# Zero products ahead of x, fewer transfers for S5's matrices, and half of the turn tables on GpSimd, in a two-layer encoder on one core

## The chip, the cores and the metric

The kernel runs on one core of a Trainium2 chip. The metric is the device time of one execution in microseconds (us); lower is better. Three runs of the kernel before took 1330.01 to 1330.89 us, median 1330.19. A profiled execution of its own is read for everything else.

## The reference

The input x has 256 tokens of 1024 channels, in float32. Two layers follow each other, and a last RMSNorm. Each layer is

```
x += 0.5 * swiglu(rms_norm(x), ffn1)                 # width 2816
h  = rms_norm(x);  split h @ w_in into S5, GLA and GQA columns
y  = [S5(u), gated linear attention, grouped-query attention]
x += (sum_b sigmoid(h @ w_merge_gate + b)_b * (y_b @ w_branch_b)) @ w_out
x += 0.5 * swiglu(rms_norm(x), ffn2)
```

The S5 branch is a linear recurrence in both directions, with 32 groups of 16 channels and 64 complex states a group: lam_bar = exp(lam dt), b_bar = (lam_bar - 1) / lam * b, state <- lam_bar * state + b_bar u, y = Re(c state). The sizes of the projections, not this recurrence, make most of the arithmetic.

## The kernel before, in words

**Products.** TensorE multiplies in a form that takes operands split into two parts. Each weight chunk (128 partitions x 2 x 512, a tile `raw`, five buffers) is loaded by SyncE's queue (L220), cast by ScalarE into `hi` (L224), and VectorE subtracts to give `lo` (L225). Three products follow for each 128x512 block: act_hi x hi (L234), act_hi x lo (L235), act_lo x hi (L236). Activations reach TensorE as hTh and hTl, made from transposes of x (class Norm, `half`). Ffn blocks are 512 columns wide, and their evacuation runs through ScalarE (L300, L306) and VectorE (L301, L307).

**Order.** Each engine executes its own list in order, and so does each DMA queue. A scheduler with a timing model lays these lists out at build time, from the order of the program, dependencies and priorities. `weave` interleaves the work that prepares S5's tables (`s5_tables`) with feed-forward layers: layer 0's with ffn1 of layer 0, layer 1's with ffn2 of layer 0 and ffn1 of layer 1.

**Start.** Under high priority the constructor issues loads of x, of the first norm's gain (`vec`) and again of x, on ScalarE's queue but for one. ScalarE also loads an activation table and runs one activation named `warm`. TensorE transposes the gain (`pv`, L189) and x (`pt`, L1169), and then the first weights products come.

**S5 tables.** `s5_params` computes powers of lam_bar, and 16 GpSimd copies (L490, L491) place one set of them as `lpb`. `s5_tables` loads the matrices B (`bn`) and C (into tiles `U`, L542), transposes C on TensorE (`cT`, L548) and copies it on ScalarE to `cq` (real, imaginary, minus imaginary). Then four quarters of 8 groups follow, in the order 1, 2, 3, 0. For each, VectorE makes `bb` (input matrices), `cc` (output matrices) and `e` (turn factors exp(i theta n), outer products of the two tables `ef` and `eg`) by complex products: four multiplications into temporaries (`T` or `U`), a subtraction and an addition, each 128x512 (`cmul_steps`, L350 to L359). GpSimd writes the decay part of `e` (L605) and four copies `kx` (L615). Quarters 1, 2 and 3 are stored in DRAM (`scr`, L612, L618) by SyncE's queue. The pool that holds `bb`, `cc` and `e` has one buffer of `e`, so the next quarter's first write to `e` waits until the store of the last has landed.

Of the kernel before, what the change touches and what calls it, by code (L numbers as in the profile page):

```python
# [9 lines left out]
F32 = mybir.dt.float32  # L10
F32R = mybir.dt.float32r
AF = mybir.ActivationFunctionType
ALU = mybir.AluOpType
AX = mybir.AxisListType

P = 128
# [12 lines left out]
NQ = 4  # L29
# [96 lines left out]
class Enc:  # L126
    def __init__(self, tc, ctx, ins, out):
        self.tc, self.nc, self.ctx, self.ins, self.out = tc, tc.nc, ctx, ins, out
        nc = self.nc
        pool = lambda name, bufs, **kw: ctx.enter_context(tc.tile_pool(name=name, bufs=bufs, **kw))  # L130
        self.const = pool("const", 1)
        self.wraw = pool("wraw", WBUFS[0])
        self.whl = pool("whl", WBUFS[1])
        self.hp = pool("hp", 1)
        self.st = pool("st", 2)
        self.pmm = pool("pmm", 3, space=bass.MemoryType.PSUM)
        self.psm = pool("psm", 3, space=bass.MemoryType.PSUM)
        self.ptr = pool("ptr", 2, space=bass.MemoryType.PSUM)
        self.n = self.ahead_by = 0
        c = self.const  # L140
        self.ident = c.tile([P, P], F32, name="ident")
        make_identity(nc, self.ident)
        self.x = c.tile([P, NT, D], F32, name="x")
        self.cst = c.tile([P, C_MIX], F32, name="cst")
        self.row = {}
        self.mhalf = c.tile([P, 32], F32, name="mhalf")
        nc.gpsimd.memset(self.mhalf, -0.5)

        nc.scalar.activation(c.tile([P, 1], F32, name="warm"), self.mhalf[:, :1], AF.Silu)
        with tc.high_priority():  # L150
            xd = lambda eng, t, h: eng.dma_start(self.x[:, t, h * 512:(h + 1) * 512],
                                                 ins["x"][0, t * P:(t + 1) * P, h * 512:(h + 1) * 512])
            xd(nc.scalar, 0, 0)
            xd(nc.sync, 1, 0)
            self.vectors("ffn1_norm", eng=nc.scalar)
            for t in range(NT):
                xd(nc.scalar, t, 1)
        self.ld = pool("s5ld", 1)
        self.ahead, self.small = {}, {}
        self.scr = {(l, q): tc.dram_tile([P, SCR], F32, name=f"scr{l}_{q}") for l in range(DEPTH) for q in range(NQ)}  # L160
# [4 lines left out]

    def t2(self, shape, dt=F32, ring="ra"):
        return self.phase.tile(shape, dt, name=self.nm("t"), tag=ring, bufs=self.rings[ring])

    def vectors(self, *names, eng=None):

# [113 lines left out]
    def ffn(self, l, which, nm, nxt):  # L284

        nc, ins = self.nc, self.ins
        wg, wu, wd = (ins[f"{which}_w_{s}"][l] for s in ("gate", "up", "down"))
        with self.tc.tile_pool(name=f"ffn{which}{l}", bufs=1) as fp:
            self.phase, self.rings = fp, {"ra": 4}
            if nm.at == 0:  # L290
                nm.half(0)
            act, rstd = nm.act, nm.rstd
            sh = fp.tile([P, KF, SEQ], F32R, name=f"sTh{which}{l}")
            sl = fp.tile([P, KF, SEQ], F32R, name=f"sTl{which}{l}")

            def evac(b):
                def f(t, ps):
                    self.n += 1
                    sg, s = self.t2([P, 256]), self.t2([P, 256])
                    nc.scalar.activation(sg, ps[:, :256], AF.Silu, scale=rstd[:, t:t + 1])  # L300
                    nc.vector.scalar_tensor_tensor(s, ps[:, 256:], rstd[:, t:t + 1], sg, op0=ALU.mult, op1=ALU.mult)  # L301
                    pt = self.ptr.tile([P, 2, P], F32, name=f"st{self.n}", tag="tr")
                    for j in range(2):
                        nc.tensor.transpose(pt[:, j], s[:, j * P:(j + 1) * P], self.ident)  # L304
                    h = sh[:, 2 * b:2 * b + 2, t * P:(t + 1) * P]
                    nc.scalar.copy(h, pt)  # L306
                    nc.vector.tensor_tensor(sl[:, 2 * b:2 * b + 2, t * P:(t + 1) * P], pt, h.bitcast(F32),  # L307
                                            op=ALU.subtract)
                return f

            blocks = []
            for b in range(KF // 2):
                cs = slice(b * 256, (b + 1) * 256)
                blocks.append((cols((wg, cs), (wu, cs)), 512, evac(b)))
            yield from self.stream(act, KD, blocks, lead=2, hooks={0: nm.finish}, fine=(l, which) == (0, "ffn1"))
            nm2 = self.nxt = nxt()
            last = isinstance(nm2, Final)

            def down(c):
                def f(t, ps):  # L320
                    xs = self.x[:, t, c * 512:(c + 1) * 512]
                    nc.vector.scalar_tensor_tensor(xs, ps, 0.5, xs, op0=ALU.mult, op1=ALU.add)
                    if last:
                        nm2.half(c, t)
                return f

            sact = lambda k, t: (sh[:, k, t * P:(t + 1) * P], sl[:, k, t * P:(t + 1) * P])
            yield from self.stream(sact, KF, [(cols((wd, slice(c * 512, (c + 1) * 512))), 512, down(c))
                                              for c in range(2)],
                                   hooks=() if last else {-(-KF // WCH) + 1: lambda: nm2.half(0)},  # L330
                                   tail=3 * WCH if last else None)
# [80 lines left out]
    def s5_params(self, l, c):  # L412
        nc, ins = self.nc, self.ins
# [14 lines left out]
        ps = self.psm.tile([P, 3, w], F32, name="lmT", tag="sm")  # L428
# [9 lines left out]
        dt, r1, cs, sn, a = (pp.tile([P, w], F32, name=f"pq{i}") for i in range(5))  # L438
# [15 lines left out]
        for i, (x, y) in {2: (1, 1), 3: (2, 1), 4: (2, 2)}.items():  # L454
            self.cmul(pw[:, 0, i], pw[:, 1, i], pw[:, 0, x], pw[:, 1, x], pw[:, 0, y], pw[:, 1, y], T)
        qo = lambda a: a.rearrange("p (q e a) -> p q e a", q=NQ, e=2)
        po = lambda a: a.rearrange("p (q a e) -> p q e a", q=NQ, e=2)
# [25 lines left out]
        pb = pp.tile([P, 2, 4, w], F32, name="pb")  # L483
# [1 line left out]
        back = [x.unsqueeze(1).to_broadcast((P, 4, w)) for x in (cs, a)]  # L485
        self.cmul(pb[:, 0], pb[:, 1], pw[:, 0, :4], pw[:, 1, :4], back[0], back[1],
                  [x.rearrange("p w f -> p (w f)").rearrange("p (f w) -> p f w", f=4) for x in T8])
        for i in range(2):
            for t in range(4):
                nc.gpsimd.tensor_copy(po(self.lpb[:64, i, t]), qo(pb[:64, i, 3 - t]))  # L490
                nc.gpsimd.tensor_copy(po(self.lpb[64:, i, t]), qo(pb[64:, i, t]))  # L491
        v.tensor_scalar(sn, sn, self.tab(C_SGN, 1), None, op0=ALU.mult)
        yield

# [20 lines left out]
    def s5_tables(self, l, pp):  # L515
        nc, ins = self.nc, self.ins
# [13 lines left out]
        cn = [T2[i].rearrange("p g c -> p (g c)").rearrange("p (t r) -> p t r", t=4) for i in range(2)]  # L530
        cq = pp.tile([P, 3, NQ, P], F32, name="cq")
        for i, s in enumerate(("re", "im")):
            bn = pp.tile([P, G, 16], F32, name=self.nm("bn"))
            b.append(bn)
            for d in range(2):
                nc.sync.dma_start(bn[d * 64:(d + 1) * 64], ins[f"s5_b_{s}"][l, d].rearrange("g p f -> p g f"))
            for d in range(2):
                for e in range(2):
                    for h in range(2):
                        for ii in range(2):  # L540
                            r = e * 64 + h * 32 + ii * 16
                            nc.sync.dma_start(  # L542
                                cn[i][r:r + 16, :, d * 64:(d + 1) * 64],
                                ins[f"s5_c_{s}"][l, d].rearrange("(h q i e) f p -> e h i f q p", q=NQ, e=2, h=2)[e, h, ii])
        for i in range(2):
            ps = self.psm.tile([P, 4, P], F32, name=self.nm("cT"), tag="sm")
            for t in range(4):
                nc.tensor.transpose(ps[:, t], cn[i][:, t], self.ident)  # L548
            nc.scalar.copy(cq[:, i], ps)
            if i == 1:  # L550
                nc.scalar.activation(cq[:, 2], ps, AF.Copy, scale=-1.0)
        yield
        T = [pp.tile([P, GQ, 4, 16], F32, name=f"T{i}") for i in range(4)]
        for q in (1, 2, 3, 0):
# [14 lines left out]
            for i in range(2):  # L569
                ps = self.psm.tile([P, 4, P], F32, name=self.nm("bT"), tag="sm")  # L570
# [15 lines left out]
            for i in range(2):  # L586
                for a in range(4):
                    for d in range(2):
                        rows = slice(d * 64, (d + 1) * 64)
                        lt = bb[rows, i, 2 * a:2 * a + 2].rearrange("p e f -> p (e f)")  # L590
                        nc.tensor.matmul(kp[d][a * 32:(a + 1) * 32, :, 1 - d:4 - d], lt, c5[rows, i, :, a, d:d + 3],
                                         start=i == 0, stop=i == 1)
# [8 lines left out]
            g8 = [self.eg[:, i, gs].unsqueeze(3).to_broadcast((P, GQ, 8, 8)) for i in range(2)]  # L601
            e8 = [E[:, i].rearrange("p g (a b) -> p g a b", a=8) for i in range(2)]
            tt = [T2[i].rearrange("p g (a b) -> p g a b", a=8) for i in range(4)]
            yield from self.cmul_steps(e8[0], e8[1], f8[0], f8[1], g8[0], g8[1], tt)
            nc.gpsimd.tensor_tensor(ld["e"][:, SCR_R - SCR_E:].rearrange("p (g c) -> p g c", g=GQ),  # L605
                                    self.r4[:, gs].unsqueeze(2).to_broadcast((P, GQ, 64)),
                                    self.tab(C_RM, 64).unsqueeze(1).to_broadcast((P, GQ, 64)), op=ALU.mult)
# [666 lines left out]
```

## Time and profile before

| | |
|---|---|
| median of three runs | 1330.19 us (1330.01 to 1330.89) |
| the profiled execution | 1329.67 us, its span 1327.9 |
| TensorE products (PE) | 1295.5 us busy, 98% |
| VectorE (DVE) | 1000.0 us, 75% |
| ScalarE (ACT) | 699.2 us, 53% |
| GpSimd (POOL) | 86.7 us, 7% |
| DMA | 249.87 MB, mean 188 GB/s |

The span runs from the first to the last recorded instruction; the execution's own time has 1.8 us more. "Busy" is the union of an engine's instructions. PEld is TensorE's weight load, which lies beside products. Products overlap in the pipeline, so their start times, not their durations, show the rate. In the timeline an arrow reads "output <- inputs", "x8" counts instructions that one row joins, and the bracket at a row's end is the time that the engine stood idle before it and what it waited for. SPq and ACTq are the issue of transfers on SyncE's and ScalarE's queue.

### The profile page before, as it was taken

To read this page: it belongs to the slowest core of one execution; us is meant where nothing else is said; L and a number is where in the kernel's file an instruction comes from. 1 tells how busy PE (TensorE), PEld (TensorE's weight loads), DVE (VectorE), ACT (ScalarE), POOL (GpSimd) and SP (SyncE) were. 2 spreads that over 40 slices of the span, in tenths; PEclk is the share of its full clock that TensorE was granted. 3 is DMA by queue.
4 is the path that set the end of the run, shared out by engine and by line. 5 is a ranking of instruction groups with operands and counts; after the bars stand their busy time and mean duration, and the time that the engine had idled before them with its cause. 6 is when DMAs were issued, how large, how long until landed. Compare 5 with 4: busy or idle time off the path is not lost.

```text
span 1327.9 us, 19275 instructions
## 1 busy us (share of the span) xinstructions
PE 1295.5 (98%) x6792; PEld 1049.2 (79%) x6792; DVE 1000.0 (75%) x1798; ACT 699.2 (53%) x1132; POOL 86.7 (7%) x109
## 2 busy tenths in 40 slices
PE   8999999999999999999999999999999999999997
PEld 6788778878787788788888778887787868888886
DVE  5899996789997678998576767557899966655553
ACT  6454455547676455554454454454485854645442
POOL 1022221000100000202010000000001000000000
PEclk9999999999999999999999999999999999999999
DMA  8775686775463367677656665566655625555661
GB/s 258 181 212 165 227 298 195 203 240 193 145 206 112 112 191 176 187 232 258 200 163 207 194 210 189 171 189 208 209 193 182 183 76 162 175 175 186 195 205 63
DMA packets 201264, 249.87 MB, mean 188 GB/s; under 512 B 40920, under 2 KB 134664, under 8 KB 201168
## 3 DMA queue, kind: packets, MB, share of 16 engines
q1 hardware_dynamic: 200416, 247.33, 59.8%
q10 hardware_dynamic: 752, 1.32, 0.3%
q8 instruction: 53, 0.87, 0.3%
q14 instruction: 43, 0.35, 0.1%
HBM read 234.44 MB, written 13.11 MB: 186 GB/s over the span
## 4 chain that ended last, share of the span: by engine, by line
PE 78%; DVE 10%; DMA 5%; issue 3%; ACT 1%; SPq 1%; POOL 0%; POOLq 0%; DVEq 0%; ACTq 0%
PE mm L234 23%; PE mm L235 23%; PE mm L236 23%; DVE lo L225 3%; DVE t L335 2%; DMA e<-scr 2%; DMA raw<-in_ffn_w_up 1%; PE st L304 1%; DVE run L834 1%; PE ao L1090 1%; SPq L220 1%; ACT hi L224 1%; PE S L816 1%; DVE run L833 1%; PE as L1068 1%
## 5 line engine op out<-in xcount | busy, mean ns | idle before, releaser
L225 DVE TENSOR_TENSOR lo<-raw,hi 128x1024 fp32r<-128x1024 f32 (+2 forms) x414 | 498.2, 1208 | 200.0 <-ACT hi L224 192.2
L224 ACT CAST hi<-raw 128x1024 fp32r<-128x1024 f32 (+2 forms) x414 | 428.6, 1039 | 340.3 <-PE mm L236 259.6
L235 PE MATMUL mm<-lo,hTh 128*128 128x512 f32 (+1 forms) x1120 | 440.0, 394 | 5.1 <-DVE lo L225 4.8
L234 PE MATMUL mm<-hi,hTh 128*128 128x512 f32 (+1 forms) x1120 | 440.2, 395 | 2.4 <-DVE gate L757 1.5
L236 PE MATMUL mm<-hi,hTl 128*128 128x512 f32 (+1 forms) x1120 | 431.4, 392 | 0.0
L235 PEld LDWEIGHTS mm<-lo,hTh 128*128 128x128 f32 x1120 | 211.0, 188 | 47.7 <-DVE lo L225 7.6
L234 PEld LDWEIGHTS mm<-hi,hTh 128*128 128x128 f32 x1120 | 211.0, 189 | 45.3 <-DVE gate L757 2.4
L236 PEld LDWEIGHTS mm<-hi,hTl 128*128 128x128 f32 x1120 | 210.5, 189 | 40.7
L235 PE MATMUL mm<-lo,sThffn 128*128 128x512 f32 x352 | 137.6, 392 | 1.2 <-DVE lo L225 1.2
L236 PE MATMUL mm<-hi,sTlffn 128*128 128x512 f32 x352 | 137.6, 392 | 0.0
L234 PE MATMUL mm<-hi,sThffn 128*128 128x512 f32 x352 | 136.2, 393 | 0.6 <-ACT hi L224 0.6
L235 PEld LDWEIGHTS mm<-lo,sThffn 128*128 128x128 f32 x352 | 66.1, 188 | 15.7 <-DVE lo L225 2.2
L234 PEld LDWEIGHTS mm<-hi,sThffn 128*128 128x128 f32 x352 | 66.1, 188 | 14.5 <-ACT hi L224 1.1
L236 PEld LDWEIGHTS mm<-hi,sTlffn 128*128 128x128 f32 x352 | 66.1, 188 | 14.0
L300 ACT ACTIVATE t<-mm,rstd 128x256 f32<-128x256 f32 x88 | 41.0, 473 | 54.6 <-PE mm L236 52.5
L306 ACT CAST sThffn<-st 128x256 fp32r<-128x256 f32 x88 | 31.5, 372 | 67.5 <-PE st L304 67.0
L307 DVE TENSOR_TENSOR sTlffn<-st,sThffn 128x256 fp32r<-128x256 f32 x88 | 35.7, 417 | 32.6 <-ACT sThffn L306 32.5
L301 DVE SCALAR_TENSOR_TENSOR t<-mm,rstd,t 128x256 f32<-128x256 f32 x88 | 40.9, 477 | 10.2 <-ACT t L300 10.0
L615 POOL COPY kx<-ks 128x128 f32<-128x128 f32 x32 | 28.1, 917 | 230.4 <-DVE ks L598 187.0
L304 PE MATMUL st<-ident,t 128*128 128x128 f32 x176 | 31.9, 274 | 0.4 <-DVE t L301 0.3
L304 PEld LDWEIGHTS st<-ident,t 128*128 128x128 f32 x176 | 23.5, 140 | 10.6 <-DVE t L301 0.7
L335 DVE TENSOR_TENSOR t<-e,S 128x512 f32<-128x512 f32 x32 | 20.3, 681 | 13.9 <-DMA e<-scr 11.2
(355 smaller groups left out, 1419.2 us busy)
## 6 DMA issues: line engine op xcount, KB each, us to landing
raw<-in_ffn_w_down SPq DMA_DIRECT2D x88, 512.0 KB, 4.7
raw<-in_ffn_w_gate SPq DMA_DIRECT2D x174, 256.0 KB, 2.9
raw<-in_ffn_w_up SPq DMA_DIRECT2D x174, 256.0 KB, 4.2
raw<-in_w_in SPq DMA_DIRECT2D x48, 512.0 KB, 4.9
raw<-in_w_merge_gate SPq DMA_DIRECT2D x48, 512.0 KB, 4.5
raw<-in_w_out SPq DMA_DIRECT2D x16, 512.0 KB, 3.9
scr<-e SPq DMA_DIRECT2D x6, 768.0 KB, 6.9
e<-scr SPq DMA_DIRECT2D x6, 768.0 KB, 6.0
```

The costliest lines, as they stand in the source:

```text
L224: nc.scalar.copy(hi[:, j:z, :width], raw[:, j:z, :width])
L225: nc.vector.tensor_tensor(lo[:, j:z, :width], raw[:, j:z, :width], hi[:, j:z, :width].bitcast(F32), op=ALU.subtract)
L234: return (nc.tensor.matmul(ps, act[0], w[0], start=first, stop=False), nc.tensor.matmul(ps, act[0], w[1], start=False, stop=False), nc.ten ...
L235: nc.tensor.matmul(ps, act[0], w[1], start=False, stop=False),
L236: nc.tensor.matmul(ps, act[1], w[0], start=False, stop=last))
L300: nc.scalar.activation(sg, ps[:, :256], AF.Silu, scale=rstd[:, t:t + 1])
L301: nc.vector.scalar_tensor_tensor(s, ps[:, 256:], rstd[:, t:t + 1], sg, op0=ALU.mult, op1=ALU.mult)
L304: nc.tensor.transpose(pt[:, j], s[:, j * P:(j + 1) * P], self.ident)
L306: nc.scalar.copy(h, pt)
L307: nc.vector.tensor_tensor(sl[:, 2 * b:2 * b + 2, t * P:(t + 1) * P], pt, h.bitcast(F32), op=ALU.subtract)
L335: self.nc.vector.tensor_tensor(out, a, b, op=ALU.mult)
L615: nc.gpsimd.tensor_copy(kx[:, :, s], ks.rearrange("p g j f -> p g (j f)")[:, :, (3 - s) * 16:(3 - s) * 16 + 64])
```

## The change

It has four parts.

1. Zero products. VectorE sets 128 columns of the tile `cst` to zero, and a new method `idle` issues f32 products of zeros on TensorE: eleven ahead of everything else, and five behind the first eight transposes of x.
2. The matrices C are loaded in 8 transfers of 64 partitions a layer instead of 32 of 16. Their channels lie in another order then, which the copies to `cq` undo (six of half the size instead of three).
3. The powers `lpb` are copied in 8 GpSimd copies of 64x64 a layer instead of 16 of 64x32.
4. In each quarter, the two products and the addition that make the imaginary half of `e` go from VectorE to GpSimd.

```diff
--- before.py
+++ after.py
@@ -147,7 +147,11 @@
         nc.gpsimd.memset(self.mhalf, -0.5)
 
         nc.scalar.activation(c.tile([P, 1], F32, name="warm"), self.mhalf[:, :1], AF.Silu)
+
+        self.zero = self.cst[:, :P]
+        nc.vector.memset(self.zero, 0.0)
         with tc.high_priority():
+            self.idle(11)
             xd = lambda eng, t, h: eng.dma_start(self.x[:, t, h * 512:(h + 1) * 512],
                                                  ins["x"][0, t * P:(t + 1) * P, h * 512:(h + 1) * 512])
             xd(nc.scalar, 0, 0)
@@ -165,6 +169,14 @@
 
     def t2(self, shape, dt=F32, ring="ra"):
         return self.phase.tile(shape, dt, name=self.nm("t"), tag=ring, bufs=self.rings[ring])
+
+    def idle(self, n, prev=None):
+
+        ps = self.pmm.tile([P, 512], F32, name=self.nm("idle"), tag="mm")
+        for _ in range(n):
+            m = self.nc.tensor.matmul(ps[:, :P], self.zero, self.zero, start=True, stop=True)
+            if prev is not None:
+                self.behind(m, prev)
 
     def vectors(self, *names, eng=None):
 
@@ -288,7 +300,7 @@
         with self.tc.tile_pool(name=f"ffn{which}{l}", bufs=1) as fp:
             self.phase, self.rings = fp, {"ra": 4}
             if nm.at == 0:
-                nm.half(0)
+                self.idle(5, nm.half(0))
             act, rstd = nm.act, nm.rstd
             sh = fp.tile([P, KF, SEQ], F32R, name=f"sTh{which}{l}")
             sl = fp.tile([P, KF, SEQ], F32R, name=f"sTl{which}{l}")
@@ -485,10 +497,12 @@
         back = [x.unsqueeze(1).to_broadcast((P, 4, w)) for x in (cs, a)]
         self.cmul(pb[:, 0], pb[:, 1], pw[:, 0, :4], pw[:, 1, :4], back[0], back[1],
                   [x.rearrange("p w f -> p (w f)").rearrange("p (f w) -> p f w", f=4) for x in T8])
-        for i in range(2):
-            for t in range(4):
-                nc.gpsimd.tensor_copy(po(self.lpb[:64, i, t]), qo(pb[:64, i, 3 - t]))
-                nc.gpsimd.tensor_copy(po(self.lpb[64:, i, t]), qo(pb[64:, i, t]))
+        for e in range(2):
+            to = self.lpb.rearrange("p i t (x e) -> p i t e x", e=2)[:, :, :, e]
+            at = pb.rearrange("p i t (q e a) -> p i t e q a", q=NQ, e=2)[:, :, :, e]
+            for i in range(2):
+                for rows, way in ((slice(0, 64), slice(None, None, -1)), (slice(64, P), slice(None))):
+                    nc.gpsimd.tensor_copy(to[rows, i].rearrange("p t (q a) -> p t q a", q=NQ), at[rows, i, way])
         v.tensor_scalar(sn, sn, self.tab(C_SGN, 1), None, op0=ALU.mult)
         yield
 
@@ -535,20 +549,21 @@
             for d in range(2):
                 nc.sync.dma_start(bn[d * 64:(d + 1) * 64], ins[f"s5_b_{s}"][l, d].rearrange("g p f -> p g f"))
             for d in range(2):
-                for e in range(2):
-                    for h in range(2):
-                        for ii in range(2):
-                            r = e * 64 + h * 32 + ii * 16
-                            nc.sync.dma_start(
-                                cn[i][r:r + 16, :, d * 64:(d + 1) * 64],
-                                ins[f"s5_c_{s}"][l, d].rearrange("(h q i e) f p -> e h i f q p", q=NQ, e=2, h=2)[e, h, ii])
+                for h in range(2):
+                    nc.sync.dma_start(
+                        cn[i][h * 64:(h + 1) * 64, :, d * 64:(d + 1) * 64],
+                        ins[f"s5_c_{s}"][l, d].rearrange("(h q x) f p -> h (x f) q p", q=NQ, h=2)[h])
         for i in range(2):
             ps = self.psm.tile([P, 4, P], F32, name=self.nm("cT"), tag="sm")
             for t in range(4):
                 nc.tensor.transpose(ps[:, t], cn[i][:, t], self.ident)
-            nc.scalar.copy(cq[:, i], ps)
-            if i == 1:
-                nc.scalar.activation(cq[:, 2], ps, AF.Copy, scale=-1.0)
+            for e in range(2):
+
+                to = lambda j: cq[:, j, :, e * 64:(e + 1) * 64].rearrange("p t (a f) -> p t a f", f=16)
+                at = ps.rearrange("p t (a e f) -> p t e a f", e=2, f=16)[:, :, e]
+                nc.scalar.copy(to(i), at)
+                if i == 1:
+                    nc.scalar.activation(to(2), at, AF.Copy, scale=-1.0)
         yield
         T = [pp.tile([P, GQ, 4, 16], F32, name=f"T{i}") for i in range(4)]
         for q in (1, 2, 3, 0):
@@ -601,7 +616,15 @@
             g8 = [self.eg[:, i, gs].unsqueeze(3).to_broadcast((P, GQ, 8, 8)) for i in range(2)]
             e8 = [E[:, i].rearrange("p g (a b) -> p g a b", a=8) for i in range(2)]
             tt = [T2[i].rearrange("p g (a b) -> p g a b", a=8) for i in range(4)]
-            yield from self.cmul_steps(e8[0], e8[1], f8[0], f8[1], g8[0], g8[1], tt)
+
+            self.mul(tt[0], f8[0], g8[0])
+            nc.gpsimd.tensor_tensor(tt[2], f8[0], g8[1], op=ALU.mult)
+            self.mul(tt[1], f8[1], g8[1])
+            nc.gpsimd.tensor_tensor(tt[3], f8[1], g8[0], op=ALU.mult)
+            yield
+            self.sub(e8[0], tt[0], tt[1])
+            nc.gpsimd.tensor_tensor(e8[1], tt[2], tt[3], op=ALU.add)
+            yield
             nc.gpsimd.tensor_tensor(ld["e"][:, SCR_R - SCR_E:].rearrange("p (g c) -> p g c", g=GQ),
                                     self.r4[:, gs].unsqueeze(2).to_broadcast((P, GQ, 64)),
                                     self.tab(C_RM, 64).unsqueeze(1).to_broadcast((P, GQ, 64)), op=ALU.mult)
```

The scheduler lays out the lists anew. Three places show how. On ScalarE at the program's start, before (`vec` is the norm's gain, `t,sq` the squares of x for the norm):

```order
L151 DMA x<-in_x 128x512
L185 DMA vec_92<-in_ffn_norm 16x128
L151 DMA x<-in_x 128x512 x2
L149 ACT_TABLE_LOAD
L149 ACTIVATE warm<-mhalf 128x1
L1176 ACTIVATE t_141,sq_117<-x 128x512
```

and after:

```order
L155 DMA x<-in_x 128x512
L149 ACT_TABLE_LOAD
L149 ACTIVATE warm<-mhalf 128x1
L197 DMA vec_105<-in_ffn_norm 16x128
L155 DMA x<-in_x 128x512 x2
L1199 ACTIVATE t_154,sq_130<-x 128x512
```

The loads of `vec` and of the second halves of x stand behind the table load and the activation `warm` now.

On VectorE in layer 0's ffn1, where the down-projection begins, before (`lo_1901` and `lo_1907` are two consecutive weight chunks; e_1509 is the second quarter's `e`, cc_1790 the third's `cc`):

```order
L225 TENSOR_TENSOR lo_1901<-raw_1898,hi_1900 128x1024
L307 TENSOR_TENSOR sTlffn_146<-st_1757,sThffn_145 128x2x128
L355 TENSOR_TENSOR e_1509<-U_1112,U_1113 128x512
L225 TENSOR_TENSOR lo_1907<-raw_1904,hi_1906 128x1024
L359 TENSOR_TENSOR e_1509<-U_1114,U_1115 128x512
L225 TENSOR_TENSOR lo_1973<-raw_1970,hi_1972 128x1024
L355 TENSOR_TENSOR cc_1790<-T_1224,T_1225 128x512
L359 TENSOR_TENSOR cc_1790<-T_1226,T_1227 128x512
```

and after, where the same two chunks are called lo_1891 and lo_1897, the second quarter's `e` e_1499 and the third's `cc` cc_1780:

```order
L237 TENSOR_TENSOR lo_1891<-raw_1888,hi_1890 128x1024
L353 TENSOR_TENSOR e_1499<-U_1123,U_1124 128x512
L367 TENSOR_TENSOR cc_1780<-T_1214,T_1215 128x512
L371 TENSOR_TENSOR cc_1780<-T_1216,T_1217 128x512
L319 TENSOR_TENSOR sTlffn_165<-st_1747,sThffn_164 128x2x128
L347 TENSOR_TENSOR U_1123<-ef,eg 128x512
L347 TENSOR_TENSOR U_1124<-ef,eg 128x512
L362 TENSOR_TENSOR T_1214<-cq,lpc 128x512
L363 TENSOR_TENSOR T_1215<-cq,lpc 128x512
L364 TENSOR_TENSOR T_1216<-cq,lpc 128x512
L366 TENSOR_TENSOR T_1217<-cq,lpc 128x512
L237 TENSOR_TENSOR lo_1897<-raw_1894,hi_1896 128x1024
```

Between the two chunks stood one 128x512 operation of the tables; nine stand there now.

On GpSimd in layer 0's tables, before (kx_1439 and kx_1775 are the first and second quarter's copies, e_1509 the second quarter's decay part):

```order
L615 COPY kx_1439<-ks_1385 128x2x64 x4
L615 COPY kx_1775<-ks_1705 128x2x64 x4
L605 TENSOR_TENSOR e_1509<-r_392,tcst 128x512
L605 TENSOR_TENSOR e_1789<-r_392,tcst 128x512
L605 TENSOR_TENSOR e_2063<-r_392,tcst 128x512
```

and after, the same copies called kx_1429 and kx_1765, with the products (L621, L623) and additions (L626) that came from VectorE:

```order
L638 COPY kx_1429<-ks_1375 128x2x64 x4
L623 TENSOR_TENSOR U_1126<-ef,eg 128x512
L621 TENSOR_TENSOR U_1125<-ef,eg 128x512
L626 TENSOR_TENSOR e_1219<-U_1125,U_1126 128x512
L621 TENSOR_TENSOR U_1125<-ef,eg 128x512
L623 TENSOR_TENSOR U_1126<-ef,eg 128x512
L638 COPY kx_1765<-ks_1695 128x2x64 x4
L626 TENSOR_TENSOR e_1499<-U_1125,U_1126 128x512
L628 TENSOR_TENSOR e_1499<-r_411,tcst 128x512
```

Two products and the addition of the first quarter and two products of the second lie between the two sets of copies now; SyncE's stores of `kx` and the weight loads behind them follow GpSimd's copies in order.

## Rows read from the trace of the kernel before

**Rows 1.** The page, part 1: busy us, share and instructions of each engine.
```profile
PE 1295.5 (98%) x6792; PEld 1049.2 (79%) x6792; DVE 1000.0 (75%) x1798; ACT 699.2 (53%) x1132; POOL 86.7 (7%) x109
```

**Rows 2.** Waits of TensorE, whole span: us, times, longest.
```profile
PE mm L235 <- DVE lo L225: 6.0, 4, 1.8
```

**Rows 3.** Timeline of TensorE, start: start us, us, instruction, [idle before].
```profile
5.64 1.97 PE L1169 MATMUL pt<-ident,x 128*128 128x128 f32 x8
8.43 1.22 PE L234 MATMUL mm<-hi,hTh 128*128 128x512 f32 x2 [0.82 <-ACT hi L224]
9.45 0.63 PE L235 MATMUL mm<-lo,hTh 128*128 128x512 f32 x1
9.87 0.63 PE L236 MATMUL mm<-hi,hTl 128*128 128x512 f32 x1
...
13.71 0.65 PE L234 MATMUL mm<-hi,hTh 128*128 128x512 f32 x2
...
17.75 0.48 PE L235 MATMUL mm<-lo,hTh 128*128 128x512 f32 x1
```

**Rows 4.** Timeline of ScalarE and its queue, start.
```profile
1.18 0.46 ACTq L185 DMA_DIRECT2D vec<-in_ffn_norm  x1
...
2.62 1.28 ACT L149 ACT_TABLE_LOAD   x1 [2.62 <-issue]
```

**Rows 5.** Timeline at the first `cT`: SyncE's queue and TensorE.
```profile
57.98 0.47 SPq L542 DMA_DIRECT2D U<-in_s_c_re  x1
...
59.28 0.39 PE L236 MATMUL mm<-hi,hTl 128*128 128x512 f32 x1
...
59.51 0.39 PE L234 MATMUL mm<-hi,hTh 128*128 128x512 f32 x1
...
61.12 0.30 PE L548 MATMUL cT<-ident,U 128*128 128x128 f32 x1 [1.23 <-DMA U<-in_s_c_re]
```

**Rows 6.** Timeline at layer 1's powers: VectorE and TensorE.
```profile
554.27 0.69 DVE L350 TENSOR_TENSOR T<-bb,lpb 128x512 f32<-128x512 f32 x1 [0.86 <-POOL lpb L491]
...
556.78 0.50 PE L235 MATMUL mm<-lo,hTh 128*128 128x512 f32 x1 [1.77 <-DVE lo L225]
```

**Rows 7.** Groups by shape, GpSimd: line, forms, count, busy us, mean ns, idle before.
```profile
L605 POOL TENSOR_TENSOR e<-r,tcst 128x512 f32<-128x512 f32 x8 | 16.4, 2050 | 165.7 <-DVE r L335 96.1 <-DMA scr<-e 59.7 <-DVE T L351 9.9
```

**Rows 8.** Timeline of GpSimd in both layers' tables.
```profile
77.20 1.06 POOL L605 TENSOR_TENSOR e<-r,tcst 128x512 f32<-128x512 f32 x1 [45.34 <-DVE r L335]
...
149.18 7.80 POOL L615 COPY kx<-ks 128x128 f32<-128x128 f32 x4 [21.44 <-DMA raw<-in_ffn_w_down]
...
181.85 3.44 POOL L605 TENSOR_TENSOR e<-r,tcst 128x512 f32<-128x512 f32 x1 [9.92 <-DVE T L351]
...
207.53 1.00 POOL L615 COPY kx<-ks 128x128 f32<-128x128 f32 x4 [18.75 <-DVE ks L598]
...
596.79 5.19 POOL L605 TENSOR_TENSOR e<-r,tcst 128x512 f32<-128x512 f32 x1 [38.73 <-DMA scr<-e]
```

**Rows 9.** Timeline of VectorE beside GpSimd's products.
```profile
157.45 2.06 DVE L225 TENSOR_TENSOR lo<-raw,hi 128x1024 fp32r<-128x1024 f32 x1
159.44 0.68 DVE L359 TENSOR_TENSOR e<-U,U 128x512 f32<-128x512 f32 x1
160.04 1.21 DVE L225 TENSOR_TENSOR lo<-raw,hi 128x1024 fp32r<-128x1024 f32 x1
...
606.89 0.69 DVE L355 TENSOR_TENSOR e<-U,U 128x512 f32<-128x512 f32 x1 [1.04 <-DMA scr<-e]
...
612.63 1.53 DVE L354 TENSOR_TENSOR U<-ef,eg 128x512 f32<-128x512 f32 x1
```

**Rows 10.** Windows of 20 us: PE, PEld, DVE, ACT, POOL busy (x instructions).
```profile
140.00:160.00 20.00, 20.00 (x121) 16.01 (x120) 20.00 (x36) 8.76 (x12) 9.25 (x5) 1.00 0.60 206
```

**Rows 11.** Timeline of TensorE at the product of `lo_1907`.
```profile
159.57 0.49 PE L235 MATMUL mm<-lo,sThffn 128*128 128x512 f32 x1
```

**Rows 12.** Waits of SyncE's queue, 100 to 215 us.
```profile
SPq L618 <- POOL kx L615: 13.1, 2, 7.6
```

## The prediction

> **What bounds the kernel now.** I read the table of engines first: TensorE (PE) is busy 1295.5 of 1327.9 us, VectorE (DVE) 1000.0, GpSimd (POOL) 86.7 [rows 1]. The end is therefore set by TensorE's work plus its gaps, some 32 us, and an edit on another engine counts only by the gap that it opens or closes. The table of waits says what the gaps are: the products with `lo` waited for VectorE's subtraction four times, 6.0 us in all [rows 2]. Then I read the timeline at the places that the diff touches. The profiled execution took 1329.67 us (1.8 us lie outside the span); the median shown is 1330.19. I add up against 1329.67 and put 0.5 us on top for the median.
>
> **Zero products.** [...] From 8.43 to 13.71 at 0.42 apart some 12.5 products are run; at 0.23 they need 2.8 us, so at most 2.45 us can be won. [...] Against it, the order on ScalarE moves: the loads of `vec` and of the second halves of x stand behind the table load, which takes 1.28 us from 2.62, and the warm-up; before, `vec` was issued at 1.18. They go out about 1.45 us later [rows 4]. Before, four us passed from the issue of `vec` to the first transpose, far more than an issue takes, so the transfers are held by each other; I charge 0.5 and not 1.45. And the next chunk's `lo`, first used at 17.75 [rows 3], hangs on its load and comes no earlier; I take off 0.35 for that, a choice. 2.45 - 0.4 - 0.5 - 0.35 = **1.2 us won**; bounds 2.5 won (nothing charged) and 1.5 lost (clock unchanged, loads late in full).
>
> [...]
>
> **C matrices.** `cT` waited 1.23 us for the load of C's real half, whose last issue stood at 57.98 on SyncE; the product before it began at 59.51, where the next is due 0.23 later, and work resumes at 61.12, so 1.4 us are lost [rows 5]. 32 transfers a layer become 8, 24 issues of 0.47 us fewer, 11 us of SyncE's time; `cT` stands at the same place in TensorE's order, and the real half goes out in 4 issues instead of 16, so its last is 12 x 0.47 = 5.6 us earlier, more than the wait. **1.4 won** (0 to 1.4). Six copies on ScalarE instead of three carry the same elements in pieces, on an engine with room: nothing.
>
> **Powers.** In layer 1, VectorE's product with `lpb` stood 0.86 us idle until GpSimd's sixteen small copies had gone far enough; the `lo` behind it came late, and TensorE stood 1.77 us before the product at 556.78 [rows 6]. With eight copies, of which six are needed, the wait should go, but the two products on VectorE before this `lo` remain. **1.5 won** (0 to 1.8). In layer 0 nothing on TensorE hung on it.
>
> **Imaginary half on GpSimd.** VectorE loses 24 operations of 128x512 at a pitch of 0.60 us (159.44 to 160.04 [rows 9]), GpSimd gains them. The nearest rows are GpSimd's own products of that shape: eight average 2.05 [rows 7], from 1.06 at 77.20 over 3.44 at 181.85 to 5.19 at 596.79 [rows 8]. Beside them VectorE is not free. The `lo` at 157.45 lasts 2.06 instead of 1.21, and a `U` at 612.63 1.53 instead of 0.68 [rows 9]: 0.85 us lost once. So it is beside six of the eight, of which these are one and the last; in the two longest GpSimd was held instead, and VectorE lost little. 6 x 0.85 / 8 = 0.64, with that little about 0.68 lost on VectorE for each GpSimd operation, against 0.60 saved. The relief is nil: a quarter of the tables costs VectorE 6 x 0.60 + 0.68 = 4.3 us before, 3 x 0.60 + 4 x 0.68 = 4.5 after (bounds: 1.8 if nothing is lost, 6.0 at 1.06, GpSimd's shortest row).
>
> [...]
>
> What is left is order. In layer 0 VectorE is busy 20.00 of the 20 us from 140 to 160 [rows 10]. Up to the `lo` called lo_1891 in the new order (lo_1901 before), VectorE has 2.9 us less to do; up to the next one (lo_1897, lo_1907 before), 1.9 more, since eight more operations at 0.60 stand between the two. I add five GpSimd operations that come before that point, 5 x 0.68 = 3.4, take off the 0.84 of the collision at 157.45, which now comes later, and 2.6 for the earlier start of everything (1.2 + 1.4). This `lo` ended at about 159.44 [rows 9], and its product began at 159.57 [rows 11], so there was no slack. Now it ends near 159.4 + 1.9 + 3.4 - 0.8 - 2.6 = 161.3, and TensorE is there at 157.0: a new gap of 4.3. Behind it TensorE had two gaps, about 1.9 us together, which a later TensorE no longer meets (the larger is among the four waits of [rows 2]). **2.5 lost** in layer 0; with no collision the new gap is 0.9 and 1.0 is won; with 1.06 each it is 6.2 and 4.3 is lost. The queues widen that upward. GpSimd's four `kx` copies took 7.80 us at 149.18 and 1.00 at 207.53 [rows 8]: GpSimd is held while VectorE runs two-input operations back to back. The `kx` of the second quarter now stands behind five more GpSimd operations, and SyncE waits for `kx` already, 13.1 us in two times [rows 12], with weights queued behind. And VectorE's `e` must wait until the quarter before has been stored, in order, as it did for 1.04 us at 606.89 [rows 9]; this `e` now stands ahead of two `lo` that it followed. High end for layer 0: 7 lost. In layer 1 the same operations meet a VectorE that stood idle there for that 1.04 us: **0.5 lost** (1 won to 4 lost).
>
> **Sum.** -1.2 - 1.4 - 1.5 + 2.5 + 0.5 = -1.1; 1329.67 - 1.1 + 0.5 = 1329.1.
>
> **Rivals.**
> *Faster: few collisions.* If VectorE and GpSimd mostly miss each other, VectorE really sheds 24 x 0.60 = 14.5 us from its fullest stretches. For it: the two longest rows, beside which VectorE lost little. Against it: the other six, and that VectorE has no gap in 140 to 160. Then layer 0 wins about 0.5 in the tables and layer 1 breaks even: -1.2 - 1.4 - 1.5 - 0.5 = -4.6, 1325.6; with the remaining `lo` gaps gone too, 1323.
> *Slower: the in-order queues.* If GpSimd's operations last as at 181.85 and 596.79, 3.4 to 5.2 us, the second quarter's `kx` ends some 4 us or more later, SyncE holds the weights behind it, and VectorE stands at `e`. Four us on the layer-0 term and three on that of layer 1 give -1.1 + 7 = +5.9, 1336; it decides from a mean of about 3.4 us. For it: `kx` at 7.80 and the 13.1 us of SyncE. Against it: five weight buffers give some cover, and only two of eight lasted so long.
> *The zero products do nothing.* The clock rises no earlier, or x is late by what ScalarE's table load takes: 1.2 to 2.7 us less won, about 1331. For it: the moved loads. Against it: TensorE busy from about 1.0 with something it had not before.
>
> **Chances.** Forecast 0.36, faster 0.31, slower 0.25, third rival 0.08. A measurement of this kernel tells about 0.2% (2.7 us) from no change; the third rival and all but 0.04 of the forecast lie inside it, so faster 0.35, same 0.40, slower 0.25. Of the likeliest case alone the range is 1327 to 1332; the whole range, with cases of both signs, is 1323 to 1335.
>
> **What would show it.** Right at the start: product spacing of 0.23 us from the first weights product, and the second `lo` product near 16.5 instead of 17.75. `cT` without a wait; no wait of VectorE on `lpb`. In 135 to 165: GpSimd operations of 1 to 5 us, each with one VectorE operation 0.85 longer, and a TensorE wait on `lo` of 2 to 6 us at the first product of lo_1897. I am wrong if VectorE's operations beside GpSimd keep 0.68 us and that wait is under 1 us, or if the clock's rise stays at 13.7.

## The result, and the profile after

The changed kernel takes 1336.93 us (1335.9 to 1339.5, five runs) against 1330.19 (1328.54 to 1330.89): a ratio of 1.0053, interval 1.0038 to 1.0067. It is slower, by 6.7 us; the forecast was 1329.1, and the range ended at 1335. The profiled execution is one of 1336.93 us with a span of 1334.7, against 1329.67 and 1327.9.

The table of engines and the waits of TensorE after (us busy; then us waited, times, longest):

```profile
PE 1300.5 (97%) x6824; PEld 1053.6 (79%) x6824; DVE 1007.2 (75%) x1775; ACT 699.4 (52%) x1138; POOL 105.5 (8%) x117
```

```profile
PE mm L247 <- DVE lo L237: 11.1, 6, 5.5
PE S L839 <- DVE t L347: 5.4, 4, 1.6
```

VectorE has 24 operations of the tables fewer (and one more, which sets the zeros) and is 7.2 us busier than in [rows 1]. TensorE's wait on `lo` went from 6.0 us to 11.1, with one of 5.5 [rows 2].

To see where, I matched the weights products of both traces one by one (4896 each, in order of time) and took the lag of the n-th:

| n | before, us | after, us | lag | what lies ahead of it |
|---|---|---|---|---|
| 14 | 14.56 | 13.27 | -1.29 | zero products |
| 190 | 57.69 | 56.80 | -0.89 | the last stretch before `cT` |
| 199 | 61.18 | 58.87 | -2.31 | `cT` |
| 480 | 132.16 | 129.82 | -2.33 | |
| 577 | 156.50 | 164.21 | +7.72 | layer 0's tables |
| 764 | 206.74 | 210.72 | +3.99 | before's own waits there |
| 1921 | 545.03 | 548.55 | +3.52 | layer 0's mixer |
| 1963 | 556.78 | 558.35 | +1.56 | powers of layer 1 |
| 2191 | 612.12 | 617.42 | +5.30 | layer 1's tables |
| 3534 | 949.55 | 956.35 | +6.80 | layer 1's mixer |

The lag at 14 counts four transposes of x that stand later in the new list; from product 30 to product 190 TensorE leads by 0.9 to 1.0 us. So it gained 0.9 at the start, 1.4 at `cT` and 2.0 at the powers; whether the parts named there made these gains is taken up below. The two stretches of tables lost 6.3 and 3.7 us. The start after, on TensorE, answers to [rows 3] (x22: a product of zeros is two records):

```profile
1.05 4.55 PE L177 MATMUL idle<-cst 128*128 128x128 f32 x22 [1.05 <-DVE cst L152]
...
5.78 1.09 PE L1192 MATMUL pt<-ident,x 128*128 128x128 f32 x8
6.71 1.28 PE L177 MATMUL idle<-cst 128*128 128x128 f32 x10
8.92 0.74 PE L246 MATMUL mm<-hi,hTh 128*128 128x512 f32 x2 [0.94 <-ACT hTh L1196]
9.50 0.62 PE L247 MATMUL mm<-lo,hTh 128*128 128x512 f32 x2
```

Behind the first, which has 0.34, products stand 0.23 apart. But the first starts 0.5 us later than in [rows 3]: it waits 0.94 us for `hTh`, which ScalarE begins at 8.40 in its new list and began at 7.41 before, and another such wait of 0.73 us follows at 11.30. The loads were not issued later: the table load, which had waited behind the issues until 2.62 [rows 4], starts at once, beside the queue:

```profile
1.18 1.28 ACT L149 ACT_TABLE_LOAD   x1 [1.18 <-PEq L1287]
...
1.24 0.39 ACTq L197 DMA_DIRECT2D vec<-in_ffn_norm  x1
```

In layer 0's tables, VectorE after, from the first stored quarter's first `U` on (two 128x512 products joined as x2):

```profile
137.64 2.75 DVE L347 TENSOR_TENSOR U<-ef,eg 128x512 f32<-128x512 f32 x2
140.32 2.31 DVE L237 TENSOR_TENSOR lo<-raw,hi 128x1024 fp32r<-128x1024 f32 x1
...
146.60 1.37 DVE L347 TENSOR_TENSOR U<-ef,eg 128x512 f32<-128x512 f32 x2
...
149.98 1.74 DVE L366 TENSOR_TENSOR T<-bb,lpb 128x512 f32<-128x512 f32 x1
151.65 2.06 DVE L237 TENSOR_TENSOR lo<-raw,hi 128x1024 fp32r<-128x1024 f32 x1
```

and GpSimd in the same stretch:

```profile
138.33 1.52 POOL L621 TENSOR_TENSOR U<-ef,eg 128x512 f32<-128x512 f32 x1
139.92 1.62 POOL L626 TENSOR_TENSOR e<-U,U 128x512 f32<-128x512 f32 x1
141.62 1.93 POOL L621 TENSOR_TENSOR U<-ef,eg 128x512 f32<-128x512 f32 x1
143.52 1.52 POOL L623 TENSOR_TENSOR U<-ef,eg 128x512 f32<-128x512 f32 x1
146.75 2.77 POOL L638 COPY kx<-ks 128x128 f32<-128x128 f32 x4 [1.71 <-DVE ks L613]
149.49 1.69 POOL L626 TENSOR_TENSOR e<-U,U 128x512 f32<-128x512 f32 x1
151.14 1.49 POOL L628 TENSOR_TENSOR e<-r,tcst 128x512 f32<-128x512 f32 x1
```

Next to a GpSimd operation the 1.22 of a `lo` becomes 2.31 and 2.06, the 0.68 of a `T` 1.74, the 1.28 of two `U` 2.75. TensorE meanwhile:

```profile
147.84 0.40 PE L246 MATMUL mm<-hi,sThffn 128*128 128x512 f32 x1
153.76 0.80 PE L247 MATMUL mm<-lo,sThffn 128*128 128x512 f32 x1 [5.52 <-DVE lo L237]
154.36 0.63 PE L248 MATMUL mm<-hi,sTlffn 128*128 128x512 f32 x1
...
158.20 0.55 PE L246 MATMUL mm<-hi,sThffn 128*128 128x512 f32 x1
158.59 0.39 PE L247 MATMUL mm<-lo,sThffn 128*128 128x512 f32 x1
```

It needs `lo_1843` at 148.07 and gets it at 153.71. Behind that wait the products stand 0.43 apart until 158.20, and only then 0.23 again: ten products, some 2 us more. The window shows a granted clock of 0.66 there (the number before the last two) and 1.00 on either side; from 154 to 158 alone it is 0.50:

```profile
140.00:150.00 10.00, 7.64 (x33) 5.66 (x31) 10.00 (x14) 3.06 (x6) 8.21 (x8) 1.00 0.58 204
150.00:160.00 10.00, 6.24 (x19) 4.94 (x20) 10.00 (x13) 1.12 (x2) 6.64 (x4) 0.66 0.52 162
160.00:170.00 10.00, 10.00 (x64) 8.06 (x63) 10.00 (x11) 5.75 (x8) 6.98 (x4) 1.00 0.57 177
```

### The profile page after: what moved, and what is told of

It is laid out like the page before. It is cut to its first block, busy times and chain, and to the rows that moved or that the text cites. A ratio compares the mean times of both kernels' runs of the same rounds, so it can differ in the third digit from the quotient of the medians.

```text
span 1334.7 us, 19282 instructions
## 1 busy us (share of the span) xinstructions
PE 1300.5 (97%) x6824; PEld 1053.6 (79%) x6824; DVE 1007.2 (75%) x1775; ACT 699.4 (52%) x1138; POOL 105.5 (8%) x117
## 4 chain that ended last, share of the span: by engine, by line
PE 45%; DVE 6%; issue 2%; DMA 1%; ACT 1%; POOLq 0%; DVEq 0%; ACTq 0%
PE mm L246 13%; PE mm L247 13%; PE mm L248 13%; DVE lo L237 1%; DVE t L347 1%; DMA e<-scr 1%; PE st L316 1%; DVE run L857 1%; DVE run L856 1%; PE ao L1113 0%; DMA bm<-in_b_merge_gate 0%; PE as L1091 0%; PE pt L1192 0%; ACT hi L236 0%; DVE U L347 0%
## 5 line engine op out<-in xcount | busy, mean ns | idle before, releaser
L237 DVE TENSOR_TENSOR lo<-raw,hi 128x1024 fp32r<-128x1024 f32 (+2 forms) x414 | 504.9, 1225 | 204.9 <-ACT hi L236 196.5
L638 POOL COPY kx<-ks 128x128 f32<-128x128 f32 x32 | 19.5, 650 | 206.8 <-DVE ks L613 191.8
L316 PEld LDWEIGHTS st<-ident,t 128*128 128x128 f32 x176 | 23.2, 141 | 11.1 <-DVE t L313 1.8
```

Source lines behind the costliest of these rows:

```text
L237: nc.vector.tensor_tensor(lo[:, j:z, :width], raw[:, j:z, :width], hi[:, j:z, :width].bitcast(F32), op=ALU.subtract)
L638: nc.gpsimd.tensor_copy(kx[:, :, s], ks.rearrange("p g j f -> p g (j f)")[:, :, (3 - s) * 16:(3 - s) * 16 + 64])
```

## The experiments

Theory A: the loss is VectorE, held by GpSimd operations that read SBUF; parts 1 to 3 keep their gains. Theory B: the loss is order, the new lists of loads and stores on SyncE's queue and what stands behind GpSimd there.

**Without part 4** (parts 1 to 3 only).

```diff
-            self.mul(tt[0], f8[0], g8[0])
-            nc.gpsimd.tensor_tensor(tt[2], f8[0], g8[1], op=ALU.mult)
...
+            yield from self.cmul_steps(e8[0], e8[1], f8[0], f8[1], g8[0], g8[1], tt)
```

> Parts 1 to 3 as in the changed kernel, the imaginary half of the turn tables back on VectorE. Theory A (the loss is VectorE held by GpSimd's reading operations; the other three parts keep what the trace shows for them, 1.3 at the start, 1.4 at cT, 2.0 at the powers): 1325 to 1327, 0.996 to 0.998 of before. Theory B (the loss comes from the new order of loads and stores on SyncE's queue and from the moved loads of x, whoever makes the tables): no better than before, 1330 to 1334.

Measured 1325.41 us, ratio 0.9961 (0.9948 to 0.9973). Repeated on another chip as the companion of a later run:

> Parts 1 to 3 once more on this chip, for the comparison with kx on ScalarE: 1325 to 1327 as before.

1326.01, 0.9965 (0.9952 to 0.9978). Parts 1 to 3 win 4 to 5 us, as A has it.

**Part 4 alone** on the kernel before (the same lines, the other way round).

> The kernel before with the imaginary half on GpSimd as the only edit. Theory A: slower than the changed kernel by what parts 1 to 3 win, 1338 to 1342. Theory B: about 1332 to 1335, since C's and the powers' lists are those of before.

1344.66 us, 1.0105 (1.0091 to 1.012): slower than either theory gave, so part 4 costs 14 us by itself and 11 on top of the others. The sum of both runs would be 1340 and not 1337, so the two do not add up; each edit lays the lists out anew, which may be why.

**Writing instead of computing.** In the changed kernel GpSimd's operations only write:

```diff
-            nc.gpsimd.tensor_tensor(tt[2], f8[0], g8[1], op=ALU.mult)
+            nc.gpsimd.memset(tt[2], 0.0)
```

(so for `tt[3]` and `e8[1]`).

> The changed kernel, but GpSimd's three operations a quarter for the imaginary half only write zeros (memset) and read nothing; the imaginary half of the tables is left out. The lists of TensorE, VectorE, ScalarE and SyncE are the same row for row. Theory A: VectorE keeps the relief without being held, its operations there take 0.68 and 1.22 again, no wait of 5.5 us on lo; 1324 to 1327. Theory B: the order is unchanged and so is most of the loss, 1333 to 1336.

> As the run with write-only operations, but three of them for each, so that GpSimd is busy about as long as in the changed kernel (some 1.5 us for each product), still without reading; the imaginary half is left out. Theory A: within 1.5 us of the run with one write for each, 1324 to 1328. Theory B in the form that GpSimd's time itself holds the stores and so the weights behind them on SyncE: 1333 to 1337, as the changed kernel.

1325.97 (0.9964, 0.995 to 0.9978; twelve executions from 1320.80 to 1332.26) and, with three writes for each, 1323.72 (0.9953, 0.9941 to 0.9965). This is the run that decides: the lists of the other four engines are the changed kernel's, and 11 to 13 us are gone. Of the run with one write each, VectorE's rows of the same stretch, GpSimd's first write to `e` there, and TensorE's product with `lo_1843`:

```profile
141.74 1.28 DVE L347 TENSOR_TENSOR U<-ef,eg 128x512 f32<-128x512 f32 x2
142.94 1.22 DVE L237 TENSOR_TENSOR lo<-raw,hi 128x1024 fp32r<-128x1024 f32 x1
...
149.72 0.69 DVE L366 TENSOR_TENSOR T<-bb,lpb 128x512 f32<-128x512 f32 x1
150.32 1.22 DVE L237 TENSOR_TENSOR lo<-raw,hi 128x1024 fp32r<-128x1024 f32 x1
...
152.25 1.24 DVE L237 TENSOR_TENSOR lo<-raw,hi 128x1024 fp32r<-128x1024 f32 x1
```

```profile
152.35 0.52 POOL L626 MEMSET e<- 128x512 f32 x1
```

```profile
151.60 0.50 PE L247 MATMUL mm<-lo,sThffn 128*128 128x512 f32 x1 [2.10 <-DVE lo L237]
```

From that first `U` to the end of `lo_1843` VectorE took 137.64 to 153.71, 16.1 us, in the changed kernel, and 141.74 to 151.54, 9.8 us, here, with the same operations in the same order. The 6.3 us between are the holding, by some eight GpSimd operations and the copies `kx`. The wait on `lo_1843` shrinks to 2.1 us, and the granted clock is 1.00 from 150 to 160, where it was 0.66. The tables of engines give the price over the whole kernel, without part 4 first, then write-only:

```profile
PE 1299.0 (98%) x6824; PEld 1053.9 (80%) x6824; DVE 999.1 (75%) x1799; ACT 699.6 (53%) x1138; POOL 78.5 (6%) x93
```

```profile
PE 1297.4 (98%) x6824; PEld 1053.2 (79%) x6824; DVE 987.0 (74%) x1775; ACT 699.2 (53%) x1138; POOL 84.4 (6%) x117
```

Part 4 takes 999.1 - 987.0 = 12.1 us off VectorE if nothing holds it, 0.50 an operation; with GpSimd reading it is 1007.2, so the holding is 20.2 us, 0.84 an operation. And the 12.1 us themselves buy next to nothing: write-only is within 2 us of the run without part 4.

The lag of the write-only run, at the products of the table above, tells which stretch is which: -2.70 at 480, -0.43 at 764, -3.09 at 1963 and -3.36 at 2191. So layer 1's tables lose nothing when GpSimd does not read, instead of 3.7, and layer 0's lose 2.3 instead of 6.3. Those 2.3 are not the moved operations holding VectorE. Two things are seen in the trace there. One is order: TensorE still waits 2.1 us for `lo_1843`, while of the two traces without part 4 one has no wait for a `lo` between 128 and 215 us and the other a single one of 0.8. The other is GpSimd being held itself. Its first four `kx` copies took 2.98 us in the changed kernel and this here, at the same place of the same VectorE list:

```profile
114.27 10.11 POOL L638 COPY kx<-ks 128x128 f32<-128x128 f32 x4 [23.25 <-DVE ks L613]
```

SyncE waited for `kx` longer than in the changed kernel (15.5 us, below), and TensorE lost some 2.5 us more than there from product 480 to 500:

```profile
SPq L641 <- POOL kx L638: 22.9, 4, 12.4
```

The run is 11 us faster all the same, so SyncE's wait behind GpSimd is not what the changed kernel lost by. A limit of the test: GpSimd's writes to `U` wait for no input and run long before their place, so the three-write run does not show what a GpSimd busy at that place, but not reading, would do.

**GpSimd in layer 1 only** (the lines of part 4 under `if l == 1`).

> The changed kernel with the imaginary half on GpSimd in layer 1 only. Theory A prices layer 1 by the trace of the changed kernel at 3.9 us (lead and lag at 560 and at 617) above parts 1 to 3: 1329 to 1331. Rival (a layer's loss is a matter of its list and not of the holding): anywhere from 1325 on, without a wait on lo between 600 and 620.

1328.51 us, 0.9992 (0.9976 to 1.0008), 2.5 above its companion without part 4 and a little below the range of either price; the two intervals just touch. In its trace, of an execution of 1332.51 us, TensorE's lag goes from -3.89 at product 1963 to +0.43 at 2191, 4.3 us, with four waits on `lo` of 0.3 to 1.0 us: about the changed kernel's 3.7 there, in an execution slower than the median.

**The other parts alone.**

> The kernel before with the zero products alone. By the trace of the changed kernel (1.3 us ahead at the fifteenth weights product) 1328.5 to 1329.2, products 0.23 us apart from the first. Rival (the start's gain is met by the next wait and lost by cT at 59 us, which hangs on a load and not on TensorE): the lead is gone behind cT, 1330.

> The kernel before with the eight transfers of C alone. cT waits for nothing, 1.4 us won: 1328.4 to 1329.2. Rival: the new lists (VectorE's and SyncE's order change with it) open another wait, 1330 or more.

> The kernel before with the eight copies of the powers alone. The wait of 1.8 us at 555 goes: 1328.1 to 1328.8. Rival: the two-input products on VectorE hold GpSimd's longer copies as they held the shorter ones, and the gain is under 0.5.

The zero products: 1329.85, 0.9984 (0.9968 to 0.9999); the lead of 1.3 at product 190, 2.0 at 199, is gone behind layer 0's tables (a lag of 0.8 at 764). C: 1327.51, 0.9973 (0.9957 to 0.9989); at `cT` its lag goes from +1.27 to -0.15, 1.4 won, and the rest of its 4 us is not explained. The powers: 1333.39, 1.001 (0.9992 to 1.0027), no gain. TensorE lags by up to 6.8 us in layer 0's tables there, though the copies of the powers take 2.74 us together. It loses 3.9 of them between products 480 and 500, behind the first `kx` copies, which took 10.11 us as in the write-only run, and 7.79 before. These are one to four us each on chips whose runs spread by more than that; only C is clear.

**Eleven zero products only,** without the five behind the transposes.

> The zero products ahead of x alone, eleven of them, without the five behind the transposes; the lists are otherwise those of the run with all sixteen. If the eleven set the clock and eight transposes hold it, weights products stand 0.23 us apart from the first one on. [...]

One execution, 1330.11 us:

```profile
1.05 5.06 PE L177 MATMUL idle<-cst 128*128 128x128 f32 x22 [1.05 <-DVE cst L152]
...
6.26 1.44 PE L1181 MATMUL pt<-ident,x 128*128 128x128 f32 x8
8.73 0.73 PE L246 MATMUL mm<-hi,hTh 128*128 128x512 f32 x2 [1.04 <-ACT hTh L1185]
9.30 0.63 PE L247 MATMUL mm<-lo,hTh 128*128 128x512 f32 x2
```

Behind the first one the weights products stand 0.23 apart without the five too, so in this execution they were not needed. The eight transposes took 1.44 us, between the 1.97 of before and the 1.09 of the changed kernel; that the clock rose while they ran, later than in the changed kernel, is an estimate from these three times. Whether the transposes had a part in the spacing is not shown: the zero products alone may have set it.

**A faster version.** Without part 4, and with `kx` copied by ScalarE:

```diff
-                nc.gpsimd.tensor_copy(kx[:, :, s], ...)
+                nc.scalar.copy(kx[:, :, s], ...)
```

> Parts 1 to 3, the imaginary half on VectorE, and the kx copies on ScalarE instead of GpSimd, so that GpSimd reads even less beside VectorE. The lists of TensorE and VectorE are those of the run with parts 1 to 3. Theory A: VectorE is held less by kx and SyncE waits less for it; 1 to 3 us faster than parts 1 to 3, 1322 to 1325. Rival: four copies a quarter push ScalarE's casts back, no gain, 1325 to 1328.

> As the run with kx on ScalarE, but the powers in sixteen short copies as before (parts 1 and 2 and kx on ScalarE). If the eight long copies win what I gave them (1.5 to 2.0 at the powers of layer 1): 1324.5 to 1325.5, with the wait near 550 back. Rival (their gain is one of the new lists, as the run with the powers alone suggests, which was no faster): 1320 to 1324.

1323.25 us, 0.9949 (0.9936 to 0.9962), the fastest with its variant with the old powers, 1323.43, 0.9951 (0.9937 to 0.9965). SyncE's wait for `kx` falls from 15.2 us (longest 9.2) without part 4 to this:

```profile
SPq L634 <- ACT kx L631: 5.8, 3, 3.3
```

Whether copied in eight or sixteen, the powers make no difference that these runs could tell.

## Why the prediction was wrong

The step that failed is the price of the imaginary half: 2.5 and 0.5 us lost in the two layers were forecast, 6.3 and 3.7 were measured. That a VectorE operation is held by some 0.85 us beside a GpSimd operation was right, with 0.84 measured; where it would meet TensorE was not. Term by term:

*Zero products,* 1.2 won: 0.9 between these two traces, and not all of it by the zero products. My bound of 2.45 took the start of one execution, products 0.42 us apart until 13.71 and 0.23 later [rows 3, 5], for that of all. That this spacing is a lower clock was an estimate from it alone: the granted clock in the trace of before is 1.00 from 8 to 14 us. The three other kernels with the old start (part 4 alone, C alone, the powers alone) came to a spacing of 0.23 at about 13.0, 11.4 and 12.3 us, not 13.7, and lead the trace of before by 0.4, 1.2 and 0.8 us at product 40 without a single zero product. C alone:

```profile
10.93 0.84 PE L234 MATMUL mm<-hi,hTh 128*128 128x512 f32 x2
11.61 0.62 PE L235 MATMUL mm<-lo,hTh 128*128 128x512 f32 x2
```

The ten traces with zero products lead by 1.0 to 1.5 there. The means of the two groups, before itself among the first, differ by some 0.5 us; that is an estimate from these fourteen traces, and about half of my term. No run shows the 0.4 that I charged for the five products behind the transposes: they took 1.28 us from 6.71, and TensorE then still stood 0.94 for `hTh`; with the eleven alone it stood 1.04. The later `hTh` had no term in it. One charge was wrong as well: the loads behind the table load in ScalarE's list go out at 1.24 as before, and the table load moves up instead.

*C,* 1.4 won: 1.4 (from -0.89 to -2.31); `cT` at 58.84 waits for nothing.

*Powers,* 1.5 won: 2.0 (from +3.52 to +1.56), and the wait is gone. But this is not shown to be the copies' doing. Every other trace gains 0.9 to 2.0 us in this stretch against the trace of before, the five with the sixteen old copies too. In two of these, C alone and `kx` on ScalarE with the old powers, VectorE stood 0.9 and 1.1 us for `lpb` as before, and TensorE waited for nothing. What else made the wait at 556.78 stays open.

*Imaginary half, layer 0,* 2.5 lost: 6.3. This went wrong in three ways. The price of a collision was 0.84 and not 0.68, as the write-only run shows; with 0.84 for five operations my sum would have risen by 0.8 only. The larger error is the sentence "TensorE is there at 157.0". I had laid VectorE's new list against TensorE's old times. TensorE's list had changed as well: the chunk called lo_1853 before, lo_1843 now, is used at 148.07 where it was used at 153.86 before:

```profile
153.86 0.39 PE L235 MATMUL mm<-lo,sThffn 128*128 128x512 f32 x1
```

TensorE came to this chunk and the three ahead of it at 145.21, 148.17, 151.14 and 153.86 before; now at 143.09, 144.45, 146.58 and 148.07, since it takes only half of each chunk's products before the next. The wait came there, two chunks earlier than I said, where VectorE had not yet shed anything: from its first `U` to the end of this `lo` it took 9.9 us before (141.54 to 151.46) and 9.8 in the write-only run. And behind the 5.5 us ten products stood 0.43 apart, with a granted clock of 0.50 from 154 to 158: 2 us for which the sum had no term. The part that I put down as given back, 1.9, was larger, 3.7 from +7.72 to +3.99: the two waits of before were 1.8 together, and 1.0 more are eight transposes of the tables that the new list has ahead of product 577. Not all of the 6.3 is the holding; the write-only run loses 2.3 here.

*Layer 1,* 0.5 lost: 3.7. I took VectorE's idle 1.04 us for slack. The write-only run loses nothing here, so this is the holding too, as in these rows of VectorE and of TensorE after:

```profile
608.42 2.60 DVE L347 TENSOR_TENSOR U<-ef,eg 128x512 f32<-128x512 f32 x2
610.95 2.09 DVE L237 TENSOR_TENSOR lo<-raw,hi 128x1024 fp32r<-128x1024 f32 x1
...
613.63 1.76 DVE L353 TENSOR_TENSOR e<-U,U 128x512 f32<-128x512 f32 x1
```

```profile
604.99 0.50 PE L247 MATMUL mm<-lo,hTh 128*128 128x512 f32 x1 [0.67 <-DVE lo L237]
...
617.42 0.50 PE L247 MATMUL mm<-lo,sThffn 128*128 128x512 f32 x1 [1.13 <-DVE lo L237]
```

*The rest.* Layer 1's mixer added 1.5 (from +5.30 to +6.80) that no part explains. TensorE's wait of `S` on VectorE's `t`, behind loads of `e`, was 5.4 us after, 5.2 without part 4 and 3.6 with `kx` on ScalarE, so it moves between kernels whose mixers are alike. All twelve other traces lose 0.5 to 2.6 us in this stretch against the trace of before, with part 4 and without, so it is not an effect of part 4; what moves it stays open. The terms as measured are -0.9 - 1.4 + 6.3 - 0.5 - 2.0 + 3.7 + 1.5 = 6.7, against 6.8 between the spans.

*The rivals.* The slower one came out near the time, 1336, but not for its reason. It was to decide from a GpSimd mean of 3.4 us; GpSimd's four kinds of eight took less, not more, than the 2.05 of [rows 7]:

```profile
L626 POOL TENSOR_TENSOR e<-U,U 128x512 f32<-128x512 f32 x8 | 16.0, 2005 | 19.7 <-DMA scr<-e 19.6
L621 POOL TENSOR_TENSOR U<-ef,eg 128x512 f32<-128x512 f32 x8 | 13.5, 1688 | 0.2
L623 POOL TENSOR_TENSOR U<-ef,eg 128x512 f32<-128x512 f32 x8 | 12.8, 1599 | 46.6 <-DVE eg L367 46.6
L628 POOL TENSOR_TENSOR e<-r,tcst 128x512 f32<-128x512 f32 x8 | 11.6, 1451 | 90.8 <-DVE r L347 90.8
```

SyncE's wait for `kx` rose only from 13.1 us [rows 12] to 15.5:

```profile
SPq L641 <- POOL kx L638: 15.5, 4, 6.6
```

and VectorE never stood at an `e` in either stretch. GpSimd was not slow; it made VectorE slow. The faster rival fell at its condition, that the two engines mostly miss each other. Behind the first one products stood 0.23 apart, so the third fell too.

A write did not hold VectorE: in the write-only run the `lo` at 152.25 took 1.24 beside a write at 152.35. Beside GpSimd operations that read, single rows were held by up to 1.1 us (the `T` at 149.98 by 1.06), and 0.84 is the mean, where GpSimd's shortest such operation is 1.06; so 1.06 was too high a price and 0.68 too low.

## What to carry to other kernels

An operation moved to another engine can cost the first engine what the second holds it up, here 0.84 us against a relief of 0.50; measure it with a twin that writes and does not read, in the same lists, before counting the relief. When a scheduler lays out all lists anew, set the new list of the engine that waits against the new list of the one that it waits for, never against the old times. And a wait can have a second price: here 5.5 us of it were followed by ten products 0.43 us apart, 2 us more.

## What the runs showed of the hardware

After waiting 5.5 us TensorE ran ten products 0.43 us apart, with a granted clock of 0.50 from 154 to 158, although in the 130 us before it had stood idle but once, for 0.6 us; after the wait of 2.1 us in the write-only run the products behind the first came 0.23 apart, with a granted clock of 1.00. The length of the wait alone does not explain these: in the run with the zero products alone eight products stood 0.43 apart behind a wait of 1.82 us, with a granted clock of 0.57 from 172 to 176:

```profile
172.37 0.67 PE L246 MATMUL mm<-hi,sThffn 128*128 128x512 f32 x1 [1.82 <-ACT hi L236]
172.83 0.63 PE L247 MATMUL mm<-lo,sThffn 128*128 128x512 f32 x1
```

Which of the two engines is held is not fixed either: the same four `kx` copies took 2.98 us in one trace and 10.11 in another beside the same VectorE operations. In the trace of before, the four that took 7.80 us [rows 8] lay beside VectorE operations with two inputs, without a gap from 149.04 to 159.44; the four that took 1.00 lay in a VectorE gap of 1.25 us that ended at 208.72. VectorE's `sTl` subtraction, which reads PSUM and SBUF, took 0.41 us beside GpSimd's products at 137.31 and 142.55 after, and 0.41 to 0.43 in all 88 of that trace; the operations held in this stretch (`U`, `lo`, `e`, `bb`, `T`) have both inputs in SBUF.
